# One large fp32 network on one core: wide passes, gates in sixteens, a moved store and a reordered latent attention

## The chip, the core and the metric

The kernel runs on one core of a Trainium2 chip. The metric is the device time of one execution in microseconds (us), lower is better. The engines are TensorE (PE for its matmuls, PEld for its weight loads), VectorE (DVE), ScalarE (ACT), GpSimd (POOL) and SyncE (SP), whose queue issues nearly all loads from HBM. Each engine works through its own instructions in the order in which the program wrote them, and waits for the others by semaphores.

## The reference, cut to what matters

256 tokens of 1024 features pass through two layers and a second block, all in float32. The parts that the change touches:

```python
mix = retention_mixer(h, ...) if i % 2 == 0 else mla_mixer(h, ...)   # layers i = 0, 1
h = layer_norm(DN_ALPHA * h + mix, ...)
h = layer_norm(DN_ALPHA * h + peer_ffn(h, w_q, sub_keys, u, v), ...)

# peer_ffn: product keys pick 16 of 16384 single-neuron experts for each of 8 heads
q = (xb @ w_q).reshape(PEER_TOKEN_BLOCK, PEER_HEADS, 2, PEER_HALF)
s = jnp.einsum('thcd,hckd->thck', q, sub_keys)        # then top 16 of 128, twice, and of the sums
h = jax.nn.gelu(jnp.einsum('thkd,td->thk', u[eidx], xb), approximate=False)
return jnp.einsum('thk,thkd->td', gate * h, v[eidx])

# mla_mixer: low-rank queries and keys, each with 64 rotated features beside 128 plain ones
c_q, c_kv, k_rope = jnp.split(x @ w_in, [384, 640], axis=-1)
q = (rms_norm(c_q, q_norm_g) @ w_uq).reshape(B, S, 8, 192)
kv = (rms_norm(c_kv, kv_norm_g) @ w_ukv).reshape(B, S, 8, 256)

# the second block: three mixers, attention to a memory of 256 rows, a feed-forward
h = h + memory_cross_attention(rmsnorm(h, ...), rmsnorm(mem, ...), xa_wq, ...)
h = h + conv_ffn(rmsnorm(h, ...), w_up, conv_w, conv_b, w_down)    # 1024 -> 2 x 2816 -> 1024
```

## The kernel before

**Products in two halves.** A float32 product is made of three faster ones. Each operand is split into a rounded half `hi` and the rest `lo` (for the activations `xh` and `xl`), and hi·xh, lo·xh and hi·xl are summed in PSUM. Weights come in chunks of 128x1024: `ws` takes one of three slots `raw` (pool `rawp`), SP loads 512 KB into it, ACT writes `hi` (`split`, L199), DVE writes `lo` = raw − hi. There are four buffers each of `hi` and `lo`. `gemm_f` (L229) turns a chunk into 128 output features of all 256 tokens: three times eight matmuls of 256 columns, weights as the stationary operand. `gemm_t` (L241) has the activations stationary and passes 512 weight columns. PSUM tiles `mm` have two buffers.

**The stages, in order.** Retention (to about 225 us): gates, queries and keys, values `vt`, attention `y` (L705), beside it the memory that the cross attention needs later (`memory_x`). Experts of layer 0 (`peer`, to 1024 us): 16 chunks of queries, the key products `scp` (L795), the search for the largest keys on DVE (`topk`), then 128 chunks of `u` and 128 of `v`. No expert is gathered: all 16384 are multiplied, and a matrix of gates picks. `gates` (L875) makes it for eight tokens at a time: DVE writes one-hot rows in float16 for four tokens, PE multiplies them (eight matmuls of 128 columns, `G`), and the same again for the other four. Latent attention (`mla`, 1038 to 1140 us): five chunks `c` with their norms and one of rotary keys `kr`; for each `c`, ACT writes a scaled copy (`cpg`, L1034) and a square (`sq`, L1037), and PE sums the squares (`ms`, L1043). Experts of layer 1 (to 1954 us). Then the mixers (to 2148 us), the cross attention (to 2216 us), the feed-forward's 44 chunks up with a convolution between (to 2342 us) and 22 down.

**What sets the order.** A tile framework places each engine's instructions by priorities and data dependencies when the program is built; `after` adds a dependency for the placement alone. `owed` is a leftover of the memory keys' norm, run by `pay` at a set column of a later stage. `Fill` puts spare matmuls `mk` of the memory keys where PE would have nothing else. Nothing is decided at run time. One ACT instruction that waits holds all behind it, and so does one load in SP's queue.

Of the kernel before, what the change touches and what calls it, by code (L numbers as in the profile page):

```python
# [38 lines left out]
FILL = 30, 8, 10  # L39
TAIL = 3  # L40
# [6 lines left out]
class Parts:  # L47


    def __init__(self, parts):  # L50
        self.parts = parts

# [3 lines left out]
    def two(self, k):  # L56
        return self.parts[k // 4][:, k % 4:k % 4 + 2]


class Fill:  # L60
# [47 lines left out]
    def rest(self):  # L108
# [9 lines left out]
        def owed():  # L118
            nc.vector.tensor_add(sq[:, 0], sq[:, 0], sq[:, 1])
            ss = K.big("xss")  # L120
            for tb in range(2):
                nc.tensor.matmul(ss[:, tb:tb + 1], sq[:, 0, tb * 128:(tb + 1) * 128], K.ones[:, 0:1], start=True, stop=True)
# [3 lines left out]
            r = K.row_scale(r)  # L126
# [3 lines left out]
        K.owed = owed  # L130


class Kern:
    def __init__(self, ctx, tc, I, out, stop=None, dbg=None):
# [6 lines left out]
        self.turned = []  # L141
        self.rawp = pool("rawp", 3)
# [58 lines left out]
    def ws(self, src, w, inner=None):  # L201
# [11 lines left out]
        ins = self.split(hi, lo, raw)  # L213
        if self.gate is not None:
# [9 lines left out]

    def gemm_f(self, out, hi, lo, xh, xl, nk, m=128):
# [8 lines left out]

    def gemm_t(self, accs, hi, lo, xh, xl, k, first, last, n=512):
# [8 lines left out]
    def rows_gemm(self, accs, nk, w, x, done=None, late=0, fill=None):  # L244
# [113 lines left out]
    def row_scale(self, r):  # L358
# [3 lines left out]
        for tb in range(2):  # L362
            R = self.t1("R")[:, :128]
            nc.vector.tensor_scalar(R, self.ones, r[:, tb:tb + 1], None, op0=OP.mult)
            nc.tensor.matmul(p[:, tb * 128:(tb + 1) * 128], R, self.ident, start=True, stop=True)
        return p

    def layer_norm(self, accs, i, page, rms=None):
# [29 lines left out]
        def done(tb):  # L398
# [35 lines left out]
            def later(first):  # L434
# [14 lines left out]
    def rms_scale(self, src, y, g, tb):  # L449
# [4 lines left out]
        for c, o in enumerate(cs):  # L454
            nc.scalar.activation(y[:, tb, o], src[:, tb, o], AF.Square, accum_out=s[:, c:c + 1])
# [3 lines left out]
        for c, o in enumerate(cs):  # L459
            nc.vector.scalar_tensor_tensor(y[:, tb, o], src[:, tb, o], s[:, 4:5], g[:, o], op0=OP.mult, op1=OP.mult)  # L460
# [103 lines left out]
    def angles(self, s, first=None):  # L564
# [176 lines left out]
    def memory_x(self):  # L741
# [5 lines left out]
        g = self.rawp.tile([128, 1024], F32, name="raw")  # L747
# [3 lines left out]
        for tb in range(2):  # L751
            self.rms_scale(m, y, g, tb)
# [3 lines left out]
            for c in range(2):  # L756
                self.turn(y[:, tb, c * 512:(c + 1) * 512], X, tb, c)
# [6 lines left out]
    def peer(self, l, rms=None):  # L764
# [95 lines left out]
    def gates(self, t0, ring, idxT):  # L860
# [3 lines left out]
        io = self.iota[:, None].to_broadcast([128, 2, 128, 2])  # L864
        for k in range(2):
# [905 lines left out]
def layout(inputs):  # L1771
# [3 lines left out]
    o = {}  # L1775
# [95 lines left out]
```

## Time and profile before

| what | value |
|---|---|
| median of 3 runs | 2421.52 us (2419.99 to 2422.97) |
| the profiled execution's own time | 2423.16 us |
| its span on the core | 2421.3 us |
| PE busy | 2390.7 us, 99% of the span |
| DVE busy | 1730.8 us, 71% |
| ACT busy | 1185.1 us, 49% |
| mean granted TensorE clock | 0.998 |

The span runs from the first to the last instruction; some 1.9 us of the execution's time lie around it. Busy is what an engine worked, shares are of the span. Matmuls overlap in PE's pipeline, so how fast they follow one another is read from their starts, not from the length of one.

### The profile page before, as it was taken

To read this page: it belongs to the slowest core of one execution; us is meant where nothing else is said; L and a number is where in the kernel's file an instruction comes from. 1 tells how busy PE (TensorE), PEld (TensorE's weight loads), DVE (VectorE), ACT (ScalarE), POOL (GpSimd) and SP (SyncE) were. 2 spreads that over 40 slices of the span, in tenths; PEclk is the share of its full clock that TensorE was granted. 3 is DMA by queue.
4 is the path that set the end of the run, shared out by engine and by line. 5 is a ranking of instruction groups with operands and counts; after the bars stand their busy time and mean duration, and the time that the engine had idled before them with its cause. 6 is when DMAs were issued, how large, how long until landed. Compare 5 with 4: busy or idle time off the path is not lost.

```text
span 2421.3 us, 40887 instructions
## 1 busy us (share of the span) xinstructions
PE 2390.7 (99%) x16220; PEld 2189.6 (90%) x16220; DVE 1730.8 (71%) x3224; ACT 1185.1 (49%) x1621; POOL 52.8 (2%) x63
## 2 busy tenths in 40 slices
PE   9999999999999999989999999999999999999999
PEld 9888999999988888888999999998888888888997
DVE  7676699888855555676599888855555678765884
ACT  4554555444444444455555444444444555444553
POOL 0000000000000000000000000000000012000000
PEclk9999999999999999999999999999999999999999
DMA  6566554444555656634645444456565755233554
GB/s 221 179 223 202 193 188 175 150 165 157 169 189 194 220 202 217 213 109 166 222 157 191 155 156 164 164 183 194 195 228 192 252 171 180 61 114 121 192 183 156
DMA packets 121391, 433.82 MB, mean 179 GB/s; under 512 B 13936, under 2 KB 14576, under 8 KB 119792
## 3 DMA queue, kind: packets, MB, share of 16 engines
q1 hardware_dynamic: 120336, 429.37, 53.0%
q8 instruction: 127, 2.08, 0.3%
q10 hardware_dynamic: 864, 1.84, 0.2%
q14 instruction: 64, 0.52, 0.1%
HBM read 424.61 MB, written 6.55 MB: 178 GB/s over the span
## 4 chain that ended last, share of the span: by engine, by line
PE 92%; DVE 4%; DMA 1%; ACT 1%; issue 1%; POOL 0%; SPq 0%; ACTq 0%; DVEq 0%
PE mm L229 44%; PE acc L241 36%; PE G L875 3%; PE acc L266 2%; DVE lo L199 1%; PE mk L95 1%; PE y L705 1%; PE scp L795 1%; ACT hi L199 1%; PE kq L229 1%; PE tp L284 1%; DMA raw<-in_mix_qk_dram 0%; PE o L1659 0%; PE pXT L1520 0%; DMA xr<-in_xT_dram 0%
## 5 line engine op out<-in xcount | busy, mean ns | idle before, releaser
L199 DVE TENSOR_TENSOR lo<-raw,hi 128x1024 fp32r<-128x1024 f32 (+2 forms) x753 | 915.1, 1218 | 458.6 <-ACT hi L199 456.6
L199 ACT ACTIVATE hi<-raw 128x1024 fp32r<-128x1024 f32 (+2 forms) x753 | 791.5, 1055 | 756.3 <-PE acc L241 300.3
L229 PE MATMUL mm<-xh,hi 128*128 128x256 f32 x3056 | 444.5, 286 | 4.4 <-DVE xl L199 2.4
L229 PE MATMUL mm<-xl,hi 128*128 128x256 f32 x3056 | 435.1, 284 | 0.0
L229 PE MATMUL mm<-xh,lo 128*128 128x256 f32 x3056 | 431.9, 284 | 0.0
L229 PEld LDWEIGHTS mm<-xh,hi 128*128 128x128 f32 x3056 | 395.8, 192 | 7.3 <-ACT xh L199 3.2
L229 PEld LDWEIGHTS mm<-xl,hi 128*128 128x128 f32 x3056 | 395.5, 192 | 0.5 <-issue 0.5
L229 PEld LDWEIGHTS mm<-xh,lo 128*128 128x128 f32 x3056 | 394.5, 192 | 0.0
L241 PE MATMUL acc<-lo,xh 128*128 128x512 f32 x1112 | 344.7, 389 | 0.0
L241 PE MATMUL acc<-hi,xh 128*128 128x512 f32 x1112 | 344.2, 389 | 0.0
L241 PE MATMUL acc<-hi,xl 128*128 128x512 f32 x1112 | 343.8, 389 | 0.0
L241 PEld LDWEIGHTS acc<-hi,xl 128*128 128x128 f32 x1112 | 208.7, 188 | 43.3
L241 PEld LDWEIGHTS acc<-lo,xh 128*128 128x128 f32 x1112 | 208.6, 188 | 43.3
L241 PEld LDWEIGHTS acc<-hi,xh 128*128 128x128 f32 x1112 | 208.5, 188 | 43.4 <-issue 0.3
L854 ACT ACTIVATE H<-mm 128x512 f32<-128x512 f32 (+30 forms) x118 | 55.2, 468 | 191.8 <-PE mm L229 191.8
L199 DVE TENSOR_TENSOR xl<-H,xh 128x1024 fp32r<-128x1024 f32 x64 | 78.2, 1224 | 48.5 <-ACT xh L199 48.5
L199 ACT ACTIVATE xh<-H 128x1024 fp32r<-128x1024 f32 x64 | 67.5, 1058 | 57.7 <-PE acc L241 56.9
L875 PE MATMUL G<-h 128*128 128x128 f16 x1024 | 78.3, 220 | 0.0
L869 DVE TENSOR_TENSOR h<-iota,idxT 128x512 f16<-128x512 f16 x128 | 53.7, 421 | 26.7 <-PE G L875 26.5
L886 DVE SCALAR_TENSOR_TENSOR H<-G,H 128x512 f32<-128x512 f32 (+26 forms) x110 | 60.2, 550 | 13.8 <-ACT H L854 13.4
L875 PEld LDWEIGHTS <-h 128*128 128x128 f16 x1024 | 59.0, 97 | 4.8
L871 DVE TENSOR_TENSOR h<-h,idxT 128x512 f16<-128x512 f16 x128 | 53.4, 419 | 0.0
(530 smaller groups left out, 2153.6 us busy)
## 6 DMA issues: line engine op xcount, KB each, us to landing
raw<-in_peer_u_dram SPq DMA_DIRECT2D x256, 512.0 KB, 3.3
raw<-in_peer_v_dram SPq DMA_DIRECT2D x256, 512.0 KB, 4.2
raw<-in_ffn_up_dram SPq DMA_DIRECT2D x44, 512.0 KB, 3.5
raw<-in_peer_q_dram SPq DMA_DIRECT2D x32, 512.0 KB, 4.3
raw<-in_ffn_down_dram SPq DMA_DIRECT2D x22, 512.0 KB, 3.5
raw<-in_ret_qk_dram SPq DMA_DIRECT2D x16, 512.0 KB, 4.4
raw<-in_ret_v_dram SPq DMA_DIRECT2D x16, 512.0 KB, 3.9
raw<-in_ret_out_dram SPq DMA_DIRECT2D x16, 512.0 KB, 4.0
```

The source lines that it names most:

```text
L95: yield nc.tensor.matmul(self.p[:, a, :], self.W[:, 2 * a + w, k * 128:(k + 1) * 128], self.X[:, k, x], start=k == 0 and j == 0, stop=k == ...
L199: return self.nc.scalar.activation(hi, src, AF.Copy), self.nc.vector.tensor_sub(lo, src, hi.bitcast(F32))
L229: ins = self.nc.tensor.matmul(out, l[:, k * m:(k + 1) * m], r[k], start=k == 0 and j == 0, stop=k == nk - 1 and j == 2)
L241: ins = self.nc.tensor.matmul(o, l, r[:, c * n:(c + 1) * n], start=first and j == 0, stop=last and j == 2)
L266: last, ins = ins, self.nc.tensor.matmul(o, l[k][:, ts], r[:, c * 512:(c + 1) * 512], start=nk <= TAIL and i == 0 and j == 0, stop=i == le ...
L284: return self.nc.tensor.transpose(out, in_, self.ident)
L705: nc.tensor.matmul(y, AT[:, h, m, n * 128:(n + 1) * 128], vt[:, m, h * 512:(h + 1) * 512], start=m == 0, stop=m == 1)
L854: nc.scalar.activation(dst[:, :, tok:], p[:, :, tok:], AF.Gelu)
L869: nc.vector.tensor_tensor(o1, io, val[0], op=OP.is_equal)
L871: nc.vector.tensor_mul(o3, o2, val[3])
L875: nc.tensor.matmul(G[:, 4 * k + t, :], o1[:, t // 2, :, t % 2], o[:, t // 2, :, t % 2], start=i == 0, stop=i == 1)
L886: nc.vector.scalar_tensor_tensor(H[:, :n, ts], Gi[:, 64 * i:64 * i + n], 1 / GS, H[:, :n, ts], op0=OP.mult, op1=OP.mult)
```

## The change

`xh` and `xl` of a chunk of activations now lie beside each other in one tile, `[128, 4, 2, 256]`. `wide` passes both in one matmul of 512 columns with `hi` as weights, and then `lo` with `xh` alone: eight matmuls of 512 and eight of 256 in place of 24 of 256, into one PSUM bank. That leaves two sums, which `pair` adds: ACT copies one half out, DVE adds the other. The first pair of each stage keeps the old way (`late`). Wide are 14 chunks of the queries in each layer of experts, 6 of the cross attention's queries and 42 of the feed-forward: 76 chunks.

The matmuls of `gates` all stand behind the last of DVE's one-hot rows, sixteen together. In the retention, the store of the table `ts` goes from SP's to ACT's queue, and the norm's gain for the memory (a row `g`) is loaded into a page instead of a `raw` slot. In the latent attention, `empties` places later weight splits behind the instructions that empty a `c` column, the rotation of the queries takes four copies on ACT and three operations on DVE in place of ten on DVE, that of the keys two and three in place of one and six, both by a weight layout that suits them, and the last three products with the values stand among the output's chunks. `owed` is paid in two steps.

```diff
+def halves_of(*pairs):
+
+    return tuple(Parts([p[:, :, i] for p in pairs], pairs) for i in range(2))
...
+        while self.emptied and self.emptied[0][0] <= self.nb - AHEAD:
+            first = self.emptied.pop(0)[1]
+            for i in ins:
+                self.after(i, first)
+        self.nb += 1
...
+    def wide(self, w, xh, xl):
+
+        hi, lo = self.ws(w, 1024)
+        p = self.mm("w").rearrange("p (a b) -> p a b", a=2)
+        for k in range(8):
+            self.nc.tensor.matmul(p, hi[:, k * 128:(k + 1) * 128], xh.both(k), start=k == 0, stop=False)
+        for k in range(8):
+            self.nc.tensor.matmul(p[:, 0], lo[:, k * 128:(k + 1) * 128], xh[k], start=False, stop=k == 7)
+        return p
+
+    def pair(self, w, xh, xl, dst=None, late=False):
+
+        if late:
+            p = self.mm().rearrange("p (a b) -> p a b", a=2)
+            for a in range(2):
+                self.gemm_f(p[:, a, :], *self.ws(w[a], 1024), xh, xl, 8)
...
+        if dst is None:
+            dst = self.t2("wd").rearrange("p (a b) -> p a b", a=2)
+        for a in range(2):
+            p = self.wide(w[a], xh, xl)
+            self.nc.scalar.activation(dst[:, a], p[:, 1], AF.Copy)
+            self.nc.vector.tensor_add(dst[:, a], p[:, 0], dst[:, a])
+        return dst
...
-            nc.sync.dma_start(self.ts, tpg[:, 3584:4096])
+
+            nc.scalar.dma_start(self.ts, tpg[:, 3584:4096])
...
-        g = self.rawp.tile([128, 1024], F32, name="raw")
+        g = y[:, 1]
...
         for c in range(0, 16, 2):
-            p = self.mm().rearrange("p (a b) -> p a b", a=2)
-            for a in range(2):
-                hi, lo = self.ws(w[l, c + a], 1024)
-                self.gemm_f(p[:, a, :], hi, lo, xh, xl, 8)
-            nc.scalar.activation(qT[:, c:c + 2], p, AF.Copy)
-            if c == 4:
+            self.pair(w[l, c:c + 2], xh, xl, qT[:, c:c + 2], late=c == 0)
+            if c in (4, 8):
                 self.pay()
...
-            nc.vector.tensor_mul(o2, o2, val[2])
-            for t in range(4):
-                for i, o in enumerate((o2, o3)):
-                    nc.tensor.matmul(G[:, 4 * k + t, :], o1[:, t // 2, :, t % 2], o[:, t // 2, :, t % 2], start=i == 0, stop=i == 1)
+            ready = nc.vector.tensor_mul(o2, o2, val[2])
+            hot.append((o1, o2, o3))
+
+        for t in (4, 5, 6, 7, 0, 1, 2, 3):
+            o1, *o = (x[:, t % 4 // 2, :, t % 2] for x in hot[t // 4])
+            for i in range(2):
+                self.after(nc.tensor.matmul(G[:, t, :], o1, o[i], start=i == 0, stop=i == 1), ready)
...
-                nc.scalar.activation(dst[0][j], p, AF.Copy, scale=self.v(gain, j))
+                self.empties(nc.scalar.activation(dst[0][j], p, AF.Copy, scale=self.v(gain, j)))
                 nc.vector.scalar_tensor_tensor(dst[1][j], p, self.v(gain, j), dst[0][j].bitcast(F32), op0=OP.mult, op1=OP.subtract)
                 sq = self.t1("sq")
-                nc.scalar.activation(sq, p, AF.Square)
+                self.empties(nc.scalar.activation(sq, p, AF.Square))
...
-            t1, t2 = self.rotated(pair(I["mla_qr"][g], 3, cqh, cql), 0)
-            for h in range(4):
-                o, s, q = 64 * (h % 2), slice(32 * h, 32 * h + 32), qr[:, 2 * g + h // 2]
-                nc.vector.tensor_sub(q[o:o + 32], t1[s, 0], t2[s, 1])
-                nc.vector.tensor_add(q[o + 32:o + 64], t2[s, 0], t1[s, 1])
+
+            p = pair(I["mla_qr"][g], 3, cqh, cql)
+            q = qr[:, 2 * g:2 * g + 2]
+            t, sw = (self.t2(n).rearrange("p (a b) -> p a b", a=2) for n in ("r1", "r2"))
+            cos, sin = (self.trig[:, i, 0][:, None, :].to_broadcast([128, 2, 256]) for i in range(2))
+            for o in (0, 64):
+                nc.scalar.activation(sw[o:o + 32], p[o + 32:o + 64], AF.Copy, scale=-1.0)
+                nc.scalar.activation(sw[o + 32:o + 64], p[o:o + 32], AF.Copy)
+            nc.vector.tensor_mul(t, p, cos)
+            nc.vector.tensor_mul(sw, sw, sin)
+            nc.vector.tensor_add(q, t, sw)
...
-                     (P, 4), (S, 6), (S, 7), (P, 5), (P, 6), (P, 7)):
+                     (P, 4), (S, 6), (S, 7)):
...
-            p = self.mm().rearrange("p (a b) -> p a b", a=2)
-            for a in range(2):
-                hi, lo = self.ws(w[a * 22 + i], 1024)
-                self.gemm_f(p[:, a, :], hi, lo, xh, xl, 8)
+            q = self.t2("q").rearrange("p (a b) -> p a b", a=2)
+            p = self.pair((w[i], w[22 + i]), xh, xl, q if i else None, late=i == 0)
```

The order of the instructions moves at three places that matter below. Before, ACT has this order at the start of the latent attention; `hi<-raw` are weight splits, `xsq` and `mkey` belong to the memory keys.

```order
L199 ACTIVATE hi<-raw 128x1024
L114 ACTIVATE xsq<-mk 128x512
L116 ACTIVATE mkey<-mk,vec 128x256 x2
L199 ACTIVATE hi<-raw 128x1024 x2
L1034 ACTIVATE cpg<-c,vec 128x256 x2
L1037 ACTIVATE sq<-c 128x256 x2
L199 ACTIVATE hi<-raw 128x1024
```

The changed kernel has this on ACT at the same place.

```order
L124 ACTIVATE xsq<-mk 128x512
L126 ACTIVATE mkey<-mk,vec 128x256 x2
L1088 ACTIVATE cpg<-c,vec 128x256 x2
L1091 ACTIVATE sq<-c 128x256
L211 ACTIVATE hi<-raw 128x1024
L1091 ACTIVATE sq<-c 128x256
L211 ACTIVATE hi<-raw 128x1024 x2
```

Two weight splits stood ahead of the copies and squares of the first two `c` columns; now the copies and the first square come first, with one split between the squares.

Before, DVE does this for two pairs of columns in the feed-forward; `q` is the scaling of a pair, `conv` the convolution and the product with the other half, `zf` a split of the result.

```order
L199 TENSOR_TENSOR lo<-raw,hi 128x1024
L1694 TENSOR_TENSOR conv<-conv,q 128x256
L1686 TENSOR_TENSOR q<-mm,rms 128x512
L199 TENSOR_TENSOR lo<-raw,hi 128x1024
L199 TENSOR_TENSOR zf_22678<-conv,zf_22678 128x256
L1691 SCALAR_TENSOR_TENSOR conv<-q,vec,conv 128x255
L1692 SCALAR_TENSOR_TENSOR conv<-q,vec,conv 128x254
L199 TENSOR_TENSOR lo<-raw,hi 128x1024
L1694 TENSOR_TENSOR conv<-conv,q 128x256
L1686 TENSOR_TENSOR q<-mm,rms 128x512
```

In the changed kernel, for one pair and a half, DVE does this; L282 is the addition in `pair`.

```order
L211 TENSOR_TENSOR lo<-raw,hi 128x1024
L211 TENSOR_TENSOR zf_22389<-conv,zf_22389 128x256
L282 TENSOR_TENSOR q<-w,q 128x256
L1746 SCALAR_TENSOR_TENSOR conv<-q,vec,conv 128x255
L1747 SCALAR_TENSOR_TENSOR conv<-q,vec,conv 128x254
L211 TENSOR_TENSOR lo<-raw,hi 128x1024
L282 TENSOR_TENSOR q<-w,q 128x256
L1749 TENSOR_TENSOR conv<-conv,q 128x256
L1741 TENSOR_TENSOR q<-q,rms 128x512
L211 TENSOR_TENSOR lo<-raw,hi 128x1024
L211 TENSOR_TENSOR zf_22389<-conv,zf_22389 128x256
```

Each chunk has an addition of its own now, and it stands right behind a weight split (and a `zf`); the scaling reads `q` itself and no longer PSUM.

Before, at the end of the experts' queries in layer 0, DVE goes from weight splits to the search for the largest keys in this way (MAX and what follows).

```order
L127 TENSOR_TENSOR mkey<-mkey,rb 128x512
L199 TENSOR_TENSOR lo<-raw,hi 128x1024 x15
L909 MAX Y<-Y 128x8 x8
L910 MAX_INDEX Y<-Y 128x8
L911 MATCH_REPLACE Y<-Y 128x128
L910 MAX_INDEX Y<-Y 128x8
L911 MATCH_REPLACE Y<-Y 128x128
L910 MAX_INDEX Y<-Y 128x8 x6
```

Now DVE has additions between the splits, and the search begins among the last chunks of queries.

```order
L282 TENSOR_TENSOR Y<-w,Y 128x256
L211 TENSOR_TENSOR lo<-raw,hi 128x1024
L282 TENSOR_TENSOR Y<-w,Y 128x256
L963 MAX Y<-Y 128x8 x8
L964 MAX_INDEX Y<-Y 128x8
L965 MATCH_REPLACE Y<-Y 128x128
L964 MAX_INDEX Y<-Y 128x8
L965 MATCH_REPLACE Y<-Y 128x128
L964 MAX_INDEX Y<-Y 128x8 x4
L211 TENSOR_TENSOR lo<-raw,hi 128x1024
L964 MAX_INDEX Y<-Y 128x8 x2
L282 TENSOR_TENSOR Y<-w,Y 128x256
```

Between two additions there now stand 18 operations of the search and one split.

## Rows read from the trace of the kernel before

**Rows 1.** The profile page: the span, busy time by engine, one costly group.

```profile
span 2421.3 us, 40887 instructions
...
PE 2390.7 (99%) x16220; PEld 2189.6 (90%) x16220; DVE 1730.8 (71%) x3224; ACT 1185.1 (49%) x1621; POOL 52.8 (2%) x63
...
L875 PE MATMUL G<-h 128*128 128x128 f16 x1024 | 78.3, 220 | 0.0
```

**Rows 2.** Waits of PE over the span: us in total, times, longest us.

```profile
PE ms L1043 <- ACT sq L1037: 5.0, 1, 5.0
...
PE y L705 <- ACT vt L684: 2.5, 1, 2.5
PE mm L229 <- DVE xl L199: 2.4, 1, 2.4
```

**Rows 3.** Timeline of PE in the feed-forward: start us, us, what.

```profile
2299.78 1.12 PE L229 MATMUL mm<-xh,hi 128*128 128x256 f32 x8
2300.74 1.12 PE L229 MATMUL mm<-xh,lo 128*128 128x256 f32 x8
```

**Rows 4.** Timeline of PE in the retention output, twelve more pairs between the two.

```profile
203.72 0.62 PE L241 MATMUL acc<-lo,zh 128*128 128x512 f32 x2
...
209.62 0.61 PE L241 MATMUL acc<-hi,zl 128*128 128x512 f32 x2
```

**Rows 5.** Timeline of PE in the experts of layer 0, a run of sixteen.

```profile
468.29 1.09 PE L875 MATMUL G<-h 128*128 128x128 f16 x16
469.19 1.20 PE L229 MATMUL mm<-xh,hi 128*128 128x256 f32 x8
470.22 1.12 PE L229 MATMUL mm<-xh,lo 128*128 128x256 f32 x8
```

**Rows 6.** Timeline of PE, same stage, a run of eight.

```profile
429.41 0.63 PE L875 MATMUL G<-h 128*128 128x128 f16 x8
429.85 1.20 PE L229 MATMUL mm<-xl,hi 128*128 128x256 f32 x8
430.89 0.40 PE L229 MATMUL mm<-xh,hi 128*128 128x256 f32 x2
```

**Rows 7.** Waits of SP's DMA queue, 60 to 130 us.

```profile
SPq L595 <- ACT trig L592: 6.1, 1, 6.1
```

**Rows 8.** Timeline of ACT in the retention; in brackets idle time before, releaser.

```profile
117.73 1.06 ACT L199 ACTIVATE hi<-raw 128x1024 fp32r<-128x1024 f32 x1 [2.80 <-DMA raw<-in_ret_g_dram]
118.69 2.04 ACT L684 ACTIVATE vt<-acc 128x512 f32<-128x512 f32 x4
```

**Rows 9.** Windows: length, busy us of PE, PEld, DVE, ACT, POOL, granted clock, DMA.

```profile
119.40:126.00 6.60, 6.60 (x21) 3.58 (x22) 5.26 (x9) 3.50 (x8) 0.55 (x1) 0.74 0.45 159
1049.10:1055.70 6.60, 6.60 (x32) 6.31 (x32) 0.00 (x0) 0.33 (x1) 0.00 (x0) 0.55 0.19 60
1964.70:1966.70 2.00, 1.97 (x16) 1.97 (x17) 2.00 (x2) 1.12 (x3) 0.00 (x0) 1.00 0.00 0
2295.31:2301.07 5.76, 5.76 (x50) 5.76 (x49) 4.69 (x7) 3.22 (x6) 0.00 (x0) 1.00 0.50 170
```

**Rows 10.** Timeline of ACT at the start of latent attention.

```profile
1045.91 1.06 ACT L199 ACTIVATE hi<-raw 128x1024 fp32r<-128x1024 f32 x1 [2.01 <-DMA raw<-in_mla_in_dram]
1046.87 0.82 ACT L1034 ACTIVATE cpg<-c,vec 128x256 fp32r<-128x256 f32 x2
1048.65 0.78 ACT L1037 ACTIVATE sq<-c 128x256 f32<-128x256 f32 x2 [0.96 <-DVE cpg L1035]
```

**Rows 11.** Groups of DVE, 2225 to 2335 us: busy us, mean ns | idle before.

```profile
L199 DVE TENSOR_TENSOR lo<-raw,hi 128x1024 fp32r<-128x1024 f32 x38 | 46.3, 1224 | 12.6 <-ACT hi L199 12.6
...
L1694 DVE TENSOR_TENSOR conv<-conv,q 128x256 f32<-128x256 f32 x17 | 7.1, 419 | 0.4 <-ACT conv L1693 0.4
```

**Rows 12.** Groups of DVE, 270 to 300 us.

```profile
L910 DVE FIND_INDEX8 Y<-Y 128x8 uint32<-128x128 f32 x16 | 4.3, 284 | 0.0
L909 DVE MAX8 Y<-Y 128x8 f32<-128x128 f32 x16 | 3.3, 276 | 0.0
```

More of the change, by code (lines that the diff above doesn't have):

```diff
@@ L47, with __init__, both @@
 class Parts:
-    def __init__(self, parts):
+    def __init__(self, parts, pairs=None):
         self.parts = parts
+        self.pairs = pairs
+    def both(self, k):
+        return self.pairs[k // 4][:, k % 4]
     def __getitem__(self, k):
@@ L121, in owed @@
             for tb in range(2):
-                nc.tensor.matmul(ss[:, tb:tb + 1], sq[:, 0, tb * 128:(tb + 1) * 128], K.ones[:, 0:1], start=True, stop=True)
+                K.after(nc.tensor.matmul(ss[:, tb:tb + 1], sq[:, 0, tb * 128:(tb + 1) * 128], K.ones[:, 0:1], start=True, stop=True), K.last)
             r = K.small(4, "kr")
@@ L242, in gemm_t, with rows_gemm @@
         return ins
-    def rows_gemm(self, accs, nk, w, x, done=None, late=0, fill=None):
+    def rows_gemm(self, accs, nk, w, x, done=None, late=0, fill=None, among={}):
         tail = []
@@ L286, in xt @@
     def xt(self):
-        q = [self.x4() for _ in range(2)]
-        return tuple(Parts([x[i] for x in q]) for i in range(2))
+        return halves_of(*(self.x4() for _ in range(2)))
     def htile(self):
@@ L356, in row_norm, with row_scale @@
         self.power(rn[:, 2 + tb:3 + tb], rn[:, tb:tb + 1], 1)
[L358 removed]
+    def row_scale(self, r, first=None):
         nc = self.nc
@@ L364, in row_scale @@
             nc.vector.tensor_scalar(R, self.ones, r[:, tb:tb + 1], None, op0=OP.mult)
-            nc.tensor.matmul(p[:, tb * 128:(tb + 1) * 128], R, self.ident, start=True, stop=True)
+            ins = nc.tensor.matmul(p[:, tb * 128:(tb + 1) * 128], R, self.ident, start=True, stop=True)
+            if first is not None:
+                self.after(ins, first)
         return p
@@ L440, in later @@
                     self.row_norm(0, y)
-                    nc.vector.scalar_tensor_tensor(y[:, 1], y[:, 1], m, gb[:, 0], op0=OP.subtract, op1=OP.mult)
+                    a = nc.vector.scalar_tensor_tensor(y[:, 1], y[:, 1], m, gb[:, 0], op0=OP.subtract, op1=OP.mult)
+                    if first is not None:
+                        self.after(a, first)
                     nc.vector.scalar_tensor_tensor(h[:, 1], y[:, 1], rs[:, 1, 1:2], gb[:, 1], op0=OP.mult, op1=OP.add)
@@ L495, in pay @@
         if self.owed is not None:
-            owed, self.owed = self.owed, None
-            owed()
+            next(self.owed, None)
     def setup(self):
@@ L824, in part @@
             if b % 4 == 0:
-                ah, al = self.x4()
-                self.split(ah, al, (H, H2)[b // 64][:, b % 64:b % 64 + 4])
-                A[0] = Parts([ah]), Parts([al])
+                A[0] = halves_of(self.x4())
+                self.split(*(x.parts[0] for x in A[0]), (H, H2)[b // 64][:, b % 64:b % 64 + 4])
             return (*A[0], b % 4)
@@ L864, in gates @@
         io = self.iota[:, None].to_broadcast([128, 2, 128, 2])
+        hot = []
         for k in range(2):
@@ L1125, in products @@
         def products(h):
-            o = self.acc("o")[:, :256]
+            o = (self.acc if h < 5 else self.big)("o")[:, :256]
             for kb in range(2):
-                nc.tensor.matmul(o, vt[:, kb, h * 128:(h + 1) * 128], PTp[:, h, kb], start=kb == 0, stop=kb == 1)
+                ins = nc.tensor.matmul(o, vt[:, kb, h * 128:(h + 1) * 128], PTp[:, h, kb], start=kb == 0, stop=kb == 1)
+                if h >= 5:
+                    self.after(ins, self.last)
             self.split(oh[h], ol[h], o)
@@ L1141, in mla @@
         self.rows_gemm(accs, 8, lambda k: I["mla_out"][k], lambda k: (oh, ol, k), self.layer_norm(accs, 1, lambda: self.page("lnp")),
-                       fill=Fill(self, 2, self.fill_pages, (0, 0, 0, 0), (1, 2)))
+                       fill=Fill(self, 2, self.fill_pages, (0, 0, 0, 0), (1, 2)), among={h - 3: lambda h=h: products(h) for h in (5, 6, 7)})
     def load(self, dst, src):
```

62 lines of the change are left out of this document (33 added, 29 removed).

## The prediction

> **What bounds the kernel now.** I read the page first: PE is busy for 2390.7 of 2421.3 us, so all of PE's idle time together is 30.6 us, and no other engine is near its limit over the whole span [rows 1]. A change can therefore save time in three ways only: fewer or quicker matmuls, less of those 30.6 us, or a higher granted clock. Next I read who PE waits for. The two longest waits of the middle of the program are one in the latent attention (5.0 us, for a square on ACT) and one in the retention (2.5 us, for the evacuation of `vt`); the mixers have one of 2.4 us [rows 2]. Then the pace of the matmuls, from their starts: eight of 256 columns every 0.96 us, 0.120 us each [rows 3]; pairs of 512 columns, 13 of them in 5.90 us, 0.454 us a pair, 0.227 us each [rows 4]. Last the granted clock. Behind the wait of 2.5 us it is 0.74 over 6.6 us, behind that of 5.0 us it is 0.55 over 6.6 us, which at 1.00 for 2.4 GHz means that much of either stretch ran at 1.2 GHz; behind the wait of 2.4 us in the mixers it stays at 1.00 [rows 9]. So a long wait is paid twice, a short one once.
>
> **Wide passes.** Per chunk 16 matmuls of 256 columns (16 × 0.120 = 1.92 us) become eight of 512 (8 × 0.227 = 1.815 us); the eight with `lo` stay. That is 0.105 us of 2.88 us per chunk, so a chunk takes 2.775 us. With 76 chunks: **8.0 us** less. Bounds: the row for 512 columns comes from products in which the activations are the weights, and no row has the weights' `hi` in that place with 512 columns. If a wide matmul costs twice a narrow one (0.240 us), the saving is nothing; more than 8.0 us no row supports. I take the measured row, since width and type are the same. The Trainium skill, "TensorE: Matmul & The Clock Gate", section "Wait — 56ns, not 53.3ns?", gives a matmul a fixed cost of about 2.5 ns beside its columns at the full clock. By that the saving would be an estimated 8 × 2.5 ns × 76 = 1.5 us. The trace disagrees here: two of 256 columns take 0.240 us and one of 512 takes 0.227 us, 13 ns apart [rows 3, 4].
>
> **Gates in sixteens.** A run of 16 `G` takes 0.90 us and one of eight 0.44 us, so the float16 products themselves cost the same per piece. But the first eight fp32 matmuls behind a run take 1.03 or 1.04 us instead of 0.96, whichever length the run had [rows 5, 6]: a switch costs about 0.075 us. I counted the runs in the order of both programs: 112 before (96 of eight, 16 of 16), 66 now. 46 switches less make **3.5 us**. The lower bound is nothing, if PE now has to wait for the later one-hot rows. It waited 0.0 us ahead of `G` before [rows 1], and each run stands eight matmuls later behind its rows, beside other matmuls that fill the time, so I take the full value.
>
> **Retention.** The wait of 2.5 us has this history: SP's queue stood 6.1 us at the store of `ts`, which needs ACT's table [rows 7]; loads behind it came late; the gain row held one of three `raw` slots; and a split on ACT that waited 2.80 us for its load stood ahead of the `vt` evacuation [rows 8]. The change takes away both the blocked queue and the lost slot. The store goes to ACT's own queue right behind the instruction that makes its data, so nothing is held there. If the loads come 2.5 us earlier, the wait goes, and with it the lost clock: 6.6 × (1 − 0.74) = 1.7 us [rows 9]. Together **4.2 us**; bound below 0, if the load of 1 MB for the memory is what fills the DMA engines, above 4.2. I take 4.2 because 6.1 us of blocked queue is more than twice what is missing.
>
> **Latent attention.** PE's 5.0 us end with the first square. Ahead of it on ACT stood two splits that waited for loads (the later one 2.01 us), then two copies, then an idle 0.96 us for DVE [rows 10]. The first square ends at 1048.65 + 0.39 = 1049.0 us; counted back 5.0 us, the second `c` column was complete, and PE idle, from 1044.0 us. In the new order the copies stand first: one copy of 0.41 us is left to do then, the square takes 0.39 us, and some 0.4 us may go for DVE's part between them. That leaves a wait of 1.2 us, so 3.8 us are saved. A wait of that length is below the 2.4 us that kept the clock, so 6.6 × (1 − 0.55) = 3.0 us come back as well [rows 9]. Together **6.8 us**. The bounds are 0 (what is late then is the load of the third chunk, which the splits wait for wherever they stand) and 8.0 (no wait at all). The rotations move work from DVE to ACT; PE's waits there are small, and I put them at nothing, with ±1.5 us.
>
> **Additions.** Wide chunks need a copy on ACT (as `cpg`, 0.41 us [rows 10]) and an addition on DVE (as an operation of the same width, 0.42 us [rows 11]). With two PSUM buffers, the addition of chunk n must be done before chunk n+2 starts, 2.775 us after n ended. In the feed-forward a split (1.22 us [rows 11]) that waits for the same chunk's `lo` buffer stands ahead of it, and on every second one a `zf` (0.42 us too): 1.22 + 0.42 + 0.42 = 2.06 us, which fits. DVE's work per pair grows from 4.69 us [rows 9] to 4.69 + 2 × 0.42 = 5.53 us, against a new period of 2 × 2.775 = 5.55 us. That is just below, so I leave PE the bound there and count nothing. In the queries of both layers of experts it does not fit at one place: from one addition to the next lie eight maxima (3.3 / 16 = 0.21 us), eight index searches (4.3 / 16 = 0.27 us) and two replacements (priced as these), 4.4 us [rows 12], a split and the addition, 6.0 us in all. The first addition ends at least 0.8 us after its chunk, and PE has two chunks of 2.775 us and a few key products ahead: about 1.0 us of waiting, **2.0 us lost** for two layers (bounds 0 and 2.6).
>
> **Sum.** 8.0 + 3.5 + 4.2 + 6.8 − 2.0 = 20.5 us. The profiled execution took 2423.16 us, which makes 2402.7; it lies 1.64 us above the median of the runs shown, so the forecast for a median is **2401.0 us**. Two medians of this kernel that are less than 0.2% (4.8 us) apart can't be told from no change.
>
> **Rivals.**
> - *DVE bounds the feed-forward.* 5.53 of 5.55 us leaves no room for waits, and DVE idles 5.76 − 4.69 = 1.07 us per pair now, mostly for ACT's `hi` [rows 9, 11]. If 0.5 us of that stays, a pair takes 6.03 us; 21 pairs lose 21 × 0.48 = 10 us: 2411 us. If 0.2 us stays, 2405 us. Against it: busy times overlap at their ends, so that DVE's real need is below their sum.
> - *The latent attention still waits.* Should the square come more than some 2.4 us late, the clock goes as well, and up to 6.8 us of the sum are missing: 2408 us. For it speaks that two loads were late there by 2 us each; against it that no split which waits for a load stands ahead of the first square.
> - *Wide saves nothing.* If time goes with columns alone, the wide stages keep their length: 2409 us. For it: the row of 512 columns has other operands in either role; against it: the 13 ns. The skill's rule above lies close to this rival, at 2401.0 + 6.5 = 2407.5 us.
> - *The other side: the hand-off of PSUM stops PE at every wide chunk.* If the addition comes later than 2.775 us behind its chunk, PE waits each time, since only two buffers are there. The margin is 0.71 us (2.775 − 2.06); beyond it every late 0.27 us per chunk eats the whole gain (20.5 / 76). DVE's two operations of the convolution ahead of the addition would be enough for that. At 0.5 us per chunk the kernel takes 2401 + 38 = 2439 us; in the feed-forward alone, 2422 us. For it: the chain of split, copy and addition is new at 76 places and DVE has no slack. Against it: the placed order has the addition ahead of the convolution.
>
> **How the numbers follow.** The forecast as it stands (2396 to 2404) gets 0.50; DVE as the bound 0.13; the latent attention 0.12; wide without gain 0.07; the hand-off 0.08, half of it above 2416; better than the forecast, since smaller waits of the 30.6 us go as well, 0.10 (2391 to 2396). The range from 2392 to 2415 leaves out some 0.1 to 0.2. Faster by over 0.2% means below 2416.7 us: all but half of the hand-off's cases and a share for what I have not seen, 0.88; within 0.2% 0.06; slower 0.06.
>
> **What would show it.** In the profile of the changed kernel: eight wide matmuls start 1.82 us before the `lo` matmuls of their chunk; runs of 16 `G`; no wait of PE for `vt`, and a clock of 1.00 behind it; a wait for `sq` near 1 us instead of 5.0, with the key chunk in 2.9 us; in the feed-forward a pair every 5.55 us, and no group of wide matmuls waiting for the addition, apart from one of about 1 us in each layer's queries. Waits of PE at wide matmuls for DVE in the feed-forward, or a low clock in the latent attention, would make the prediction wrong.

## The result and the profile after

The changed kernel takes 2442.94 us (median of 5, 2442.0 to 2447.43) against 2421.52 us, a ratio of 1.0094 with a 95% interval of 1.008 to 1.0108. It is slower by 21 us, where 2401 us was forecast. The profiled execution is the one of 2442.94 us.

First the page of the changed kernel, span and busy times.

```profile
span 2441.2 us, 39800 instructions
...
PE 2389.8 (98%) x15612; PEld 2163.2 (89%) x15612; DVE 1748.0 (72%) x3283; ACT 1210.3 (50%) x1692; POOL 55.6 (2%) x63
```

PE worked 0.9 us less than before and idled 51.4 us (2441.2 − 2389.8) instead of 30.6 [rows 1]. So new waits are the first thing to look for. The waits of PE over the span:

```profile
PE mm L252 <- ACT e L907: 19.7, 8, 4.3
...
PE rb L416 <- DVE R L415: 1.9, 1, 1.9
...
PE G L929 <- DVE h L923: 1.6, 2, 0.9
...
PE acc L291 <- ACT x L211: 1.3, 2, 0.7
PE w L263 <- DVE Y L282: 1.3, 3, 0.5
...
PE w L263 <- DVE wd L282: 1.3, 1, 1.3
PE w L263 <- DVE q L1741: 1.2, 1, 1.2
...
PE w L263 <- ACT qp L1696: 0.9, 1, 0.9
PE ms L1099 <- ACT sq L1091: 0.8, 1, 0.8
```

The old waits for `sq` and `vt` [rows 2] have gone or shrunk to 0.8 us, as forecast. The third wait of [rows 2], 2.4 us for `xl` at the head of the mixers, is gone too, but 1.9 us for `R`, 14 us further on, stand in its place. On top stands a new one: matmuls `mm` that wait for `e` on ACT, 19.7 us in 8 places. `e` is the gelu of the experts' `u` chunks for tokens whose gates are made already (function `blocks`): ACT reads a PSUM tile into a buffer `e` (two of them), DVE multiplies it into `H`, and only when ACT has read the tile may PE reuse it. The gates (`G`) are made in the same stretch from one-hot rows that DVE writes into a ring of 8 slots, three slots for every four tokens. Three views of the same stretch show who holds whom. The timeline of PE in the changed kernel (start, length, what, idle before; the last row is cut by the window):

```profile
601.41 1.09 PE L929 MATMUL G<-h 128*128 128x128 f16 x16
...
607.57 1.22 PE L252 MATMUL mm<-x,hi 128*128 128x256 f32 x8 [2.39 <-ACT e L907]
...
610.79 1.09 PE L929 MATMUL G<-h 128*128 128x128 f16 x16
...
617.00 2.08 PE L252 MATMUL mm<-x,hi 128*128 128x256 f32 x8 [2.44 <-ACT e L907]
...
621.66 0.52 PE L929 MATMUL G<-h 128*128 128x128 f16 x6
```

The timeline of ACT, with the same columns:

```profile
607.03 0.49 ACT L907 ACTIVATE e<-mm 128x384 f32<-128x384 f32 x1 [0.60 <-DVE H L908]
...
616.45 1.04 ACT L907 ACTIVATE e<-mm 128x400 f32<-128x400 f32 x2 [0.65 <-DVE H L908]
```

The timeline of DVE, where L923 is the last one-hot row of a run of gates, L920 the first of the next, and L908 the product with `e`:

```profile
598.16 0.42 DVE L923 TENSOR_TENSOR h<-h,idxT 128x512 f16<-128x512 f16 x1
...
602.03 0.43 DVE L920 TENSOR_TENSOR h<-iota,idxT 128x512 f16<-128x512 f16 x1 [1.05 <-PE G L929]
...
606.46 0.54 DVE L908 TENSOR_TENSOR H<-H,e 128x368 f32<-128x368 f32 x1
...
608.04 0.43 DVE L923 TENSOR_TENSOR h<-h,idxT 128x512 f16<-128x512 f16 x1
611.41 0.42 DVE L920 TENSOR_TENSOR h<-iota,idxT 128x512 f16<-128x512 f16 x1 [2.94 <-PE G L929]
...
615.86 1.03 DVE L908 TENSOR_TENSOR H<-H,e 128x384 f32<-128x384 f32 x2
...
622.27 0.42 DVE L920 TENSOR_TENSOR h<-iota,idxT 128x512 f16<-128x512 f16 x1 [3.92 <-PE G L929]
...
632.25 0.42 DVE L920 TENSOR_TENSOR h<-iota,idxT 128x512 f16<-128x512 f16 x1 [1.58 <-PE G L929]
```

Read it as a ring. The last one-hot row is written at 598.6 us, and the sixteen `G` stand at 601.4 us in PE's order. DVE cannot start the next rows before they have run (1.05 us idle, released by `G`). Behind those rows in DVE's order stands the product with `e` (606.46). ACT's next `e` waits for it (0.60 us), PE waits for ACT's `e` (2.39 us), and the next sixteen `G` stand behind that in PE's order, at 610.8 us. Once more around, DVE idles 2.94 us and PE 2.44 us; a third time DVE idles 3.92 us, and then the ring loosens (1.58 us). A round takes 9.4 and then 10.9 us. A run of gates is due every 2.5 chunks (`GR`), which with 2.88 us for a chunk and 0.97 us for the run and the slower matmuls behind it [rows 5] makes 8.2 us.

The wait of DVE for `G` was there before the change, shorter. The waits of DVE from 380 to 720 us (in all, times, longest), in the kernel before:

```profile
DVE h L869 <- PE G L875: 13.2, 19, 0.9
```

And in the changed kernel, over the same stretch:

```profile
DVE h L920 <- PE G L929: 24.5, 19, 3.9
```

The longest was 0.9 us and is now 3.9 us. Last the windows of the changed kernel (length, busy us of PE, PEld, DVE, ACT, POOL, clock):

```profile
617.00:622.00 5.00, 5.00 (x32) 4.96 (x33) 1.35 (x2) 0.87 (x2) 0.00 (x0) 0.67 0.49 183
684.60:691.00 6.40, 6.34 (x40) 6.35 (x41) 1.97 (x3) 1.66 (x3) 0.00 (x0) 0.73 0.02 8
1056.00:1060.00 4.00, 4.00 (x34) 3.90 (x34) 3.27 (x4) 3.98 (x5) 0.00 (x0) 1.00 0.32 109
118.50:125.00 6.50, 6.50 (x36) 4.59 (x35) 4.89 (x12) 2.25 (x6) 1.50 (x3) 1.00 0.49 159
2262.00:2350.00 88.00, 87.41 (x498) 76.75 (x499) 82.45 (x142) 61.94 (x112) 0.00 (x0) 1.00 0.58 194
```

Behind two of the new waits of layer 0 the clock falls (0.67 and 0.73), so they are paid twice; in layer 1 it falls behind two as well (0.66 from 1538 to 1543 us, 0.55 from 1615 to 1621 us). In the latent attention and behind the `vt` evacuation it holds at 1.00, where it was 0.55 and 0.74 [rows 9]. The retention has no wait left ahead of `y`:

```profile
118.16 0.47 PE L252 MATMUL mm<-x,hi 128*128 128x256 f32 x1
118.47 2.74 PE L760 MATMUL y<-vt,atp 128*128 128x512 f32 x6
```

And the latent attention now waits 0.84 us for the first square, and its key chunk takes 2.9 us (1056.79 to 1059.72):

```profile
1054.04 1.12 PE L252 MATMUL c<-x,hi 128*128 128x256 f32 x8
1056.00 0.61 PE L1099 MATMUL ms<-ones,sq 128*128 128x1 f32 x4 [0.84 <-ACT sq L1091]
...
1056.79 1.28 PE L252 MATMUL kr<-x,hi 128*64 128x256 f32 x8
...
1059.72 0.50 PE L1099 MATMUL ms<-ones,sq 128*128 128x1 f32 x4
```

**Stage by stage.** The table gives the length of each stage in us, worked out from the timelines of PE: from the start of its first matmul, less the idle time just ahead of it, to that of the next stage. (At the latent attention, where that idle time is 0.2 us in all of them, it is left in.) Column names are those of the experiments below.

| stage | before | after | e1 | e2 | e3 | e4 | e5 | e9 | e11 | e12 |
|---|---|---|---|---|---|---|---|---|---|---|
| start, to `y` | 116.8 | 118.5 | 118.1 | 116.8 | 118.3 | 116.5 | 118.0 | 117.8 | 117.0 | 117.8 |
| retention from `y` | 108.9 | 104.5 | 104.5 | 108.9 | 108.6 | 104.7 | 104.5 | 104.5 | 104.5 | 104.5 |
| queries and `u`, layer 0 | 456.1 | 469.2 | 456.8 | 477.2 | 456.9 | 457.1 | 456.1 | 456.1 | 456.3 | 456.1 |
| `v`, layer 0 | 356.2 | 357.0 | 357.0 | 356.2 | 357.0 | 356.2 | 356.2 | 356.2 | 357.0 | 356.2 |
| latent attention | 112.2 | 103.2 | 104.0 | 111.6 | 111.7 | 103.6 | 111.5 | 103.2 | 103.3 | 104.1 |
| queries and `u`, layer 1 | 456.1 | 471.4 | 456.5 | 477.7 | 457.4 | 456.7 | 456.1 | 456.2 | 456.5 | 456.3 |
| `v`, layer 1 | 356.0 | 356.8 | 356.8 | 356.0 | 356.8 | 356.0 | 356.0 | 356.0 | 356.8 | 356.0 |
| mixers | 199.5 | 200.7 | 200.5 | 200.7 | 199.3 | 200.5 | 200.9 | 200.5 | 199.0 | 200.7 |
| cross attention | 67.4 | 69.7 | 69.5 | 67.4 | 69.9 | 67.3 | 67.3 | 67.5 | 67.3 | 67.3 |
| feed-forward | 187.9 | 186.2 | 186.3 | 187.9 | 185.9 | 187.9 | 187.9 | 187.9 | 186.5 | 186.3 |

The two stages with gates lose 13.1 and 15.3 us; the rest together gains 8.3 us.

### The profile page after: what moved, and what is told of

Read it like the earlier page. It is cut to its first block, busy times and chain, and to the rows that moved or that the text cites. A ratio compares the mean times of both kernels' runs of the same rounds, so it can differ in the third digit from the quotient of the medians.

```text
span 2441.2 us, 39800 instructions
## 1 busy us (share of the span) xinstructions
PE 2389.8 (98%) x15612; PEld 2163.2 (89%) x15612; DVE 1748.0 (72%) x3283; ACT 1210.3 (50%) x1692; POOL 55.6 (2%) x63
## 4 chain that ended last, share of the span: by engine, by line
PE 47%; DVE 4%; ACT 2%; DMA 2%; issue 1%; POOL 0%; POOLq 0%; ACTq 0%; DVEq 0%
PE acc L291 19%; PE mm L252 15%; PE w L263 4%; PE w L265 2%; PE acc L320 2%; DVE lo L211 1%; PE G L929 1%; DMA raw<-in_peer_q_dram 1%; ACT hi L211 1%; DMA raw<-in_xa_wq_dram 0%; DMA raw<-in_ffn_up_dram 0%; PE o L1185 0%; PE mk L105 0%; PE pXT L1581 0%; ACT x L211 0%
## 5 line engine op out<-in xcount | busy, mean ns | idle before, releaser
L252 PE MATMUL mm<-x,hi 128*128 128x256 f32 x4896 | 662.6, 286 | 22.5 <-ACT e L907 19.7
L252 PEld LDWEIGHTS mm<-x,hi 128*128 128x128 f32 x4896 | 619.4, 193 | 27.5 <-ACT e L907 21.2
L291 PE MATMUL acc<-hi,x 128*128 128x512 f32 x2224 | 598.0, 389 | 1.3 <-ACT x L211 1.3
L291 PEld LDWEIGHTS acc<-hi,x 128*128 128x128 f32 x2224 | 417.2, 188 | 88.7 <-ACT x L211 1.7
L252 PE MATMUL mm<-x,lo 128*128 128x256 f32 x2448 | 351.8, 286 | 0.0
L291 PE MATMUL acc<-lo,x 128*128 128x512 f32 x1112 | 344.2, 389 | 0.0
L252 PEld LDWEIGHTS mm<-x,lo 128*128 128x128 f32 x2448 | 321.1, 194 | 0.2
L291 PEld LDWEIGHTS acc<-lo,x 128*128 128x128 f32 x1112 | 208.6, 188 | 43.1
L263 PE MATMUL w<-x,hi 128*128 128x512 f32 x608 | 155.8, 398 | 4.9 <-DVE Y L282 1.3
L263 PEld LDWEIGHTS w<-x,hi 128*128 128x128 f32 x608 | 109.1, 189 | 26.2 <-DVE Y L282 1.9
L920 DVE TENSOR_TENSOR h<-iota,idxT 128x512 f16<-128x512 f16 x128 | 53.8, 422 | 48.4 <-PE G L929 48.2
```

The lines of the kernel that those rows point to most:

```text
L252: ins = self.nc.tensor.matmul(out, l[:, k * m:(k + 1) * m], r[k], start=k == 0 and j == 0, stop=k == nk - 1 and j == 2)
L263: self.nc.tensor.matmul(p, hi[:, k * 128:(k + 1) * 128], xh.both(k), start=k == 0, stop=False)
L291: ins = self.nc.tensor.matmul(o, l, r[:, c * n:(c + 1) * n], start=first and j == 0, stop=last and j == 2)
L920: nc.vector.tensor_tensor(o1, io, val[0], op=OP.is_equal)
```

## The experiments

Each ratio is to the kernel before on the same chip. One line of the diff, an `after` in `layer_norm`, is in no experiment by itself: the changed kernel, e1, e10 and e11 have it, the others do without.

**e1, the changed kernel with eights.** Undone is this part alone:

```diff
-        hot = []
...
-            ready = nc.vector.tensor_mul(o2, o2, val[2])
-            hot.append((o1, o2, o3))
-
-        for t in (4, 5, 6, 7, 0, 1, 2, 3):
-            o1, *o = (x[:, t % 4 // 2, :, t % 2] for x in hot[t // 4])
-            for i in range(2):
-                self.after(nc.tensor.matmul(G[:, t, :], o1, o[i], start=i == 0, stop=i == 1), ready)
+            nc.vector.tensor_mul(o2, o2, val[2])
+            for t in range(4):
+                for i, o in enumerate((o2, o3)):
+                    nc.tensor.matmul(G[:, 4 * k + t, :], o1[:, t // 2, :, t % 2], o[:, t // 2, :, t % 2], start=i == 0, stop=i == 1)
```

> The changed kernel with the gates' matmuls in runs of eight again, each behind its own half of the one-hot rows; all else as changed. Theory G (the sixteens hold PE in the experts): the changed kernel idles 11.4 and 11.2 us in the two layers' expert blocks for the gelu `e` and for `h`, and its clock is low in four places there (8.5 us lost); all of that goes and the 3.5 us of the switches come back: 2443 - 22.6 - 8.5 + 3.5 = about 2415 us, and no wait of PE for `e`. Theory Q (the wide queries and the earlier search shift the whole placement of the expert blocks, the sixteens are not the cause): the waits stay and the time is 2438 to 2446 us.

2415.95 us, ratio 0.9978 (0.9969 to 0.9987): 27.0 us below the changed kernel. PE has no wait for `e` left, and the two stages take 456.8 and 456.5 us. Theory G holds.

**e2, the kernel before with sixteens.** The same edit the other way.

> The kernel before with only the gates' matmuls in sixteens. Theory G: waits of PE for `e` of some 20 us in all appear, with low clock behind them: 2421.5 + 22.6 + 8.5 - 3.5 = about 2449 us. Theory Q: no such waits, and the switches saved: 2418 us.

2461.81 us, ratio 1.0173 (1.0159 to 1.0187), 41 us more, even above what theory G gave. PE's wait for `e` is there:

```profile
PE mm L229 <- ACT e L857: 25.2, 9, 4.3
```

The two stages lose 21.1 and 21.6 us. Why the sixteens cost 41 us alone and 27 us among the other parts is open. A possible reason, not tested: the layers' runs stand at other places among the chunks, and each round in which PE waits can lose clock or not.

**e3, the kernel before with wide passes** (the diff's `wide`, `pair`, `halves_of` and their callers).

> The kernel before with only the wide passes (76 chunks). Theory W (a wide chunk takes 0.105 us less, waits for the addition cost some 5 us in the queries, the cross attention and at the first wide chunk of the feed-forward): 2421.5 - 8 + 5 = about 2418 us. Theory Q: the expert blocks wait as in the changed kernel: 2435 us or more.

2426.43 us, ratio 1.0025 (1.0015 to 1.0035): no 3 us less, but 5.6 us more. Theory Q is out, the stages with gates take 456.9 and 457.4 us; theory W has the wrong sign. By the stages: the feed-forward gains 2.0 us, the cross attention loses 2.5, the two queries 0.8 and 1.3, the two `v` stages 0.8 each, and the start 1.5 us (its granted clock from 10 to 12 us is 0.50, against 1.00 in the profile of before).

**e4, the kernel before with the latent attention's part.**

> The kernel before with only the latent attention's part: order of the copies, rotations, products among the output's chunks, the leftover norm paid in two steps. The stage from the first `c` to the queries of layer 1 took 112.2 us before and 103.2 us in the changed kernel. If that gain is this part's own: 2421.5 - 9 = 2412.5 us, less up to 1 us. If it comes in part from the other parts (the two layers' norm and fill ahead of it): 2415 to 2419 us.

2415.56 us, ratio 0.9977 (0.9968 to 0.9987), 5.3 us less. The stage takes 103.6 instead of 112.2 us, so the gain is this part's own; the difference to the median is in small losses elsewhere (0.6 to 1.0 us in each `u` stage and in the mixers) and in the profiled execution, which had no wait for `vt` either and, at 2412.21 us, was the fastest of the ten. That `vt` wait is missing although e4 has the retention of the kernel before. SP's queue stands at the store of `ts` in e4 too, but the last split ahead of the `vt` evacuation waits 1.48 us for its load, where it was 2.80 us [rows 8]. The wait of SP's queue in e4:

```profile
SPq L614 <- ACT trig L611: 4.9, 1, 4.9
```

The timeline of ACT in e4:

```profile
114.88 1.06 ACT L202 ACTIVATE hi<-raw 128x1024 fp32r<-128x1024 f32 x1 [1.48 <-DMA raw<-in_ret_g_dram]
115.85 2.04 ACT L703 ACTIVATE vt<-acc 128x512 f32<-128x512 f32 x4
```

**e5, the kernel before with the retention's part.**

> The kernel before with only the retention's part: the store of `ts` on ACT's queue, the gain row in a page instead of a raw slot. Theory L (that queue and that slot made the load late on which the evacuation of `vt` waits): no wait of PE for `vt`, clock 1.00 behind it, 2420.9 - 4.2 = about 2416.7 us. Theory D (the DMA engines are full of the memory's 1 MB there, and when the loads land changes from run to run): the wait stays at 1 to 2.5 us or comes and goes, 2419 to 2421 us.

2419.4 us, ratio 0.9993 (0.9984 to 1.0002): no difference that can be told from none. The wait for `vt` is gone and the retention takes 104.5 instead of 108.9 us, as theory L has it, but 1.2 us are lost at the start and 1.4 us in the mixers, and the median falls by 1.5 us only. That time lies in theory D's range, not at L's 2416.7 us, and the runs don't decide between the two: all seven profiled kernels with this part (the changed one, e1, e5, e9 to e12) have no wait for `vt`, the kernel before, e2 and e3 have 2.2 to 2.5 us, but e4 has none without the part. If the wait comes and goes between executions of the kernel before too, the part can save less in a median than in one profile; no run shows how often it comes. In the mixers, PE's timeline of e5:

```profile
1960.83 1.70 PE L229 MATMUL mm<-xh,hi 128*128 128x256 f32 x8 [2.41 <-DVE xl L199]
```

The window of e5 behind this wait:

```profile
1962.00:1968.00 6.00, 6.00 (x42) 6.00 (x42) 5.92 (x7) 2.25 (x4) 0.00 (x0) 0.77 0.70 212
```

The wait is as long as before (2.41 us, against 2.4 us [rows 2]), but this time the clock over the stretch behind it is 0.77, where it was 1.00 [rows 9].

**e6, e7, e8, more slots for one-hot rows.** A larger ring needs room, so all three have three buffers of `hi` and `lo` instead of four; e6 is that base with eights, e7 has sixteens and 8 slots, e8 sixteens and 16 slots.

```diff
-TAIL = 3
+TAIL = 2
...
-            o1, o2, o3 = (ring[:, (ts.start // 4 * 3 + i) % 8] for i in range(3))
+            o1, o2, o3 = (ring[(ts.start // 4 * 3 + i) % 16] for i in range(3))
```

> The base for the next two: the kernel before with three buffers each of `hi` and `lo` instead of four (and tails of two chunks instead of three), which frees 8 KB per partition. Both theories: PE is fed with one chunk less ahead, 2421 to 2450 us, no wait for the gelu `e` in the experts.

> The same with the gates in sixteens and the ring of 8 slots for one-hot rows. Both theories: as between the kernel before and the one with sixteens alone, some 40 us above the base with three buffers, with waits of PE for `e`.

> The same with the gates in sixteens and a ring of 16 slots. Theory R (a run of sixteen holds 6 of 8 slots until all have run, so DVE waits for G before it can write the next one-hot rows, and what stands behind them on DVE, the product with `e`, is late): with 16 slots DVE does not wait for G, the waits for `e` go, and the time is 3 us below the base with three buffers. Theory P (the sixteen stand too late in PE's order because they need the last of eight one-hot rows; slots do not matter): as with 8 slots, some 40 us above the base.

The base takes 2435.93 us (ratio 1.0056, 1.0041 to 1.0071), with 8 slots 2453.06 us (1.0134, 1.0119 to 1.015), with 16 slots 2432.02 us (1.0042, 1.0028 to 1.0056). PE waits for `e` in e7 only, and in e6 and e8 nowhere:

```profile
PE mm L229 <- ACT e L857: 7.5, 4, 3.0
```

DVE's waits for `G` from 380 to 720 us, first in e7 (in e8 half of the slots are called `ring`):

```profile
DVE h L870 <- PE G L879: 22.0, 22, 1.5
```

The same view of e8:

```profile
DVE h L872 <- PE G L880: 3.2, 4, 1.0
DVE ring L872 <- PE G L880: 3.0, 4, 1.0
```

22.0 us against 3.2 + 3.0 = 6.2 us. Theory R holds, and theory P is out: e7 and e8 have the sixteen matmuls behind the last one-hot row alike, and with room for two whole runs PE's waits for `e` go and DVE's for `G` fall below those of e6 (13.5 us). The two stages with gates then take 456.6 and 457.5 us, against 458.3 and 458.8 in e6, so the sixteens save 1.7 and 1.3 us, together 3.0 us and near the 3.5 us forecast for them. The medians (3.9 us apart) can't show this by themselves: their intervals overlap, and in the profiled executions the two `v` stages, which have no gates, differ by 2.0 and 1.9 us as well. With 8 slots the sixteens cost 17 us here rather than the 40 expected.

**e9, retention and latent attention together, no wide passes, eights.**

> The kernel before with the retention's and the latent attention's part, neither wide passes nor sixteens. Theory A (the two parts act in stages apart and add up): 2420.9 - 1.5 - 5.3 = about 2414 us. Theory B (part of what one saves comes back as a lower clock in another stage, since a wait and its clock are moved): 2415.5 us, no better than the latent attention's part alone.

2412.55 us, ratio 0.9962 (0.9949 to 0.9976). Theory A holds, and the time is 1.5 us better than the sum.

**e10 and e11, where wide passes lose.** e10 is e1 with `late=True` in the cross attention, e11 has it in the experts' queries as well, so that only the feed-forward is wide.

> The changed kernel with eights, and the cross attention's queries the old way. Theory H (two PSUM buffers hold PE there until copy and addition are done, 2.4 us in the trace, more than the six wide chunks save): 2.0 to 2.4 us below the one with eights alone, so 2416 - 2.3 = about 2413.5 us. Theory C (the cross attention is longer for another reason, as the layout of the activations): no change, 2416 us.

> The same with the experts' queries the old way too: wide passes in the feed-forward alone. Theory H: the queries' stages lose 0.5 to 1.3 us less per layer, so about 2412 us, the lowest of all. Theory C: the experts' stages stay as long as with wide queries (456.8 us from the queries to the `v` chunks of layer 0), 2416 us.

e10 takes 2413.85 us (0.9965, 0.9952 to 0.9979), 2.1 us below e1, and its cross attention takes 67.3 instead of 69.5 us: theory H. e11 takes 2412.77 us (0.9964, 0.995 to 0.9977), another 1.1 us, which the medians alone could not show. The queries and `u` of layer 0 take 456.3 us (456.8 in e1), at the low end of theory H; those of layer 1 stay at 456.5 us, as theory C has it. In the changed kernel, PE waits at two wide chunks of the cross attention:

```profile
2191.01 2.11 PE L263 MATMUL w<-x,hi 128*128 128x512 f32 x8 [0.86 <-ACT qp L1696]
...
2197.53 2.11 PE L263 MATMUL w<-x,hi 128*128 128x512 f32 x8 [1.28 <-DVE wd L282]
```

The first waits for ACT, which reads the PSUM tile of the old-style first pair in three passes; the second waits for the addition of the chunk before it.

**e12, the parts that gain.** This is the retention's and the latent attention's part with wide passes in the feed-forward alone, and only the feed-forward's activations lie beside each other.

```diff
+                if i == 2:
+                    xp = self.pages.tile([128, 8, 2, 256], F32R, name="ffnx", tag="pg")
+                    self.xh, self.xl = halves_of(xp[:, 0:4], xp[:, 4:8])
+                else:
+                    self.xh, self.xl = self.xt()
```

> The kernel before with the retention's and the latent attention's part and wide passes in the feed-forward alone; only the feed-forward's activations lie beside each other, in a page, all other tiles stay apart. Theory H (all that is lost with wide passes lies in hand-offs of PSUM and in the shared tile of activations): the experts' `v` stages take 356.2 and 356.0 us again, the feed-forward 186 us instead of 187.9 us: 2412.6 - 1.9 = about 2410.7 us. Theory C (the gain of wide passes in the feed-forward is eaten by waits elsewhere): 2412 to 2413 us.

2410.97 us, ratio 0.9959 (0.9946 to 0.9973), the lowest of all, and the `v` stages are at 356.2 and 356.0 us: their 0.8 us came from the shared tile. Between e9 and e12 the medians differ by less than they can tell; the feed-forward's 187.9 and 186.3 us show it.

## Why the prediction was wrong, point by point

**Gates in sixteens** is the step that failed, with the wrong sign: −3.5 us forecast, +27.0 us measured (after against e1). The mechanism of the gain is there, the two stages of e8 show 3.0 us. What I missed is the other side of the ring: sixteen matmuls hold 6 of 8 slots, so DVE waits for PE in its own order, and behind DVE's wait stand the products that ACT and then PE wait for (DVE's waits for `G` from 13.2 to 24.5 us in layer 0, PE 19.7 us for `e` in both layers). I asked only whether PE would wait for DVE, read that it waited 0.0 us for `h` [rows 1], and set the lower bound at nothing. The trace of before had the warning in DVE's waits: 19 waits for `G`, 13.2 us. With half a run held, they were short enough; I did not look there. The bound below should have been a loss, priced by the round.

**Wide passes.** Three terms were off. The gain per chunk is 0.085 us, not 0.105, as the feed-forward of the changed kernel shows (columns as above):

```profile
2302.06 2.00 PE L263 MATMUL w<-x,hi 128*128 128x512 f32 x8
2303.90 1.12 PE L265 MATMUL w<-x,lo 128*128 128x256 f32 x8
2304.86 2.00 PE L263 MATMUL w<-x,hi 128*128 128x512 f32 x8
...
2307.65 2.00 PE L263 MATMUL w<-x,hi 128*128 128x512 f32 x8
```

Two chunks in 5.59 us make 2.795 us, and a wide matmul takes 0.230 us (1.84 / 8). That makes 76 × 0.085 = 6.5 us instead of 8.0. The rival in which it saves nothing fell. The estimate of 1.5 us by the Trainium skill, "TensorE: Matmul & The Clock Gate", section "Wait — 56ns, not 53.3ns?", fell too: merging two matmuls of 256 columns into one took 10 ns off (2 × 0.120 − 0.230 us), not the 2.5 ns of fixed cost that is stated there. In the queries the key products `scp` stand between the chunks now, and the eight wide matmuls behind each are slower:

```profile
251.87 0.61 PE L846 MATMUL scp<-Y 128*128 128x128 f32 x4
252.28 2.11 PE L263 MATMUL w<-x,hi 128*128 128x512 f32 x8
254.23 1.12 PE L265 MATMUL w<-x,lo 128*128 128x256 f32 x8
```

They take 1.95 us here and 1.93 us at most other places, instead of 1.84. With that the gain of 14 chunks per layer (1.2 us) is about used up, and waits for additions of 0.3 to 0.7 us come on top, where I had put 1.0 us. In the cross attention I counted no hand-off; it cost more (2.1 us, e10) than six chunks save (0.5 us). And the shared tile of activations, which I gave no price, costs 0.8 us at the head of each `v` stage, as e12 shows: one half of a tile is not written while PE still reads the other, and PE then waits up to 0.7 us for ACT's `x`. Of forecast −8.0 + 2.0 = −6.0 us, +5.6 us were measured (e3); some 1.5 us of that may be the start, where the clock fell in e3 and not in the profile of before.

**Latent attention** was right in kind and near in size: 0.84 us of wait are left (1.2 forecast), the clock is 1.00, the stage is 9.0 us shorter in the changed kernel, and e4's median 5.3 us lower, against a forecast of 6.8 us.

**Retention** was right in the stage (4.4 us, forecast 4.2) and not in the total: 1.5 us in e5's median, within the noise. In e5's profile the rest went into the start and the mixers, where the clock fell. I took the `vt` wait of one execution for a fixed cost; e4 shows that the same code can do without it, so the 4.2 us may not be there to be saved each time. That a 2.4 us wait keeps the clock was read from one place in one execution as well.

**DVE as the bound of the feed-forward** did not come: PE is busy 87.41 of 88.00 us there, with DVE at 82.45 (94%). One wait of 1.2 us stands at its head, at the first wide chunk behind the old-style pair.

**The other side** was forecast with the wrong mechanism: PE waits 4.9 us in all at wide matmuls, at a few places, not at each of 76 chunks. It was the gates' ring that decided. That this rival's 2439 us lies near the 2442.94 us measured is chance.

## What to carry to other kernels

Where matmuls are put into longer runs, count what buffers the run holds until its end, and ask who waits for those; a sign of it stands in the waits of the engine that fills them, not in those of the busiest one. When an order is closed into a ring over three engines, a wait can come back and grow for some rounds (here 1.05, 2.94 and 3.92 us on DVE) instead of being paid once. In this kernel a merged pass paid in a long stretch of equal chunks, the feed-forward; in the cross attention its hand-off cost more (2.1 us) than the six chunks there gain (0.5 us). And a wait for a load that stands in one profile should be looked for in a second one before its removal is priced.

## What the runs showed of the hardware that I had not expected

A wait of PE of 2.4 us was followed by the full clock in the kernel before (1964.7 us, 1.00) and by 0.77 in e5 at the same place after 2.41 us. In the changed kernel a wait of 2.39 us (607.57) cost no clock, eight matmuls behind it took 1.22 us, and one of 2.44 us (617.00) did, the eight took 2.08 us. So some 1.4 to 1.7 us per such place (6.0 × 0.23, 5.0 × 0.33) come and go, in e5 with no change in the code near it. This may be a part of the 2418 to 2424 us over which the kernel before spreads; only one execution of that kernel was profiled, so it is not shown. And eight wide matmuls behind a few fp32 products take 0.09 to 0.11 us longer, much as the fp32 matmuls behind float16 ones did [rows 5, 6].
